# Stores and loads moved to another queue, one product and some sums moved in the order, and one tile given its own buffers, in a one-core encoder trunk

## The chip, the core and the metric

One core of one Trainium2 chip. The program runs alone on it. The metric is device time in microseconds (us) of one execution; below, "the runs" are repeated executions of the same program, and the trace is of one further execution, taken by the hardware profiler.

Names of engines: PE is the matrix engine (its clock is granted by a throttle, which the profile shows), DVE the vector engine, ACT the scalar engine, POOL GpSimd, SP the engine that only issues DMAs. POOL and ACT can issue DMAs too; a DMA stands in the instruction queue of the engine that issues it, in order with that engine's other work.

## The reference

Two groups of 512 tokens of width 1024 (`x_prompt`, `x_sample`) go through one encoder layer with shared weights. In short:

```python
h = rmsnorm(x, g_mix);  u = h @ w_in
qk, v, o, gates, c_q, c_kv, k_r, gm = split(u)          # gm: 2 x 1024 columns, the merge gates
y_m = (sigmoid(o) * rmsnorm(mlstm(qk, v, gates))) @ w_mo  # matrix memory, both directions
y_a = attention(rmsnorm(c_q) @ w_uq, rmsnorm(c_kv) @ w_ukv, k_r) @ w_ao   # 8 heads, rotary part
g_m, g_a = split(sigmoid(gm))
x = x + (g_m * y_m + g_a * y_a) @ w_out
h2 = rmsnorm(x, g_ffn)
x = x + (silu(h2 @ w_gate) * (h2 @ w_up)) @ w_down
x = x + sigmoid(x @ w_ple_gate) * (p @ w_ple)
y = rmsnorm(x, g_final)
```

All is float32.

## The kernel before

**Matmuls.** Data lie with the feature on the 128 partitions and the 512 tokens of a group along the free dimension. A float32 product is made of three matmuls: each operand is split into a high part (a cast, on ACT) and a low part (the rest, a subtraction, on DVE, line 168 in the helper `lo_of`), and high x high, high x low and low x high are summed in PSUM. So every operand costs one ACT instruction and one DVE instruction before PE can use it.

**Seven products for eight.** Where two column blocks of a weight meet the two groups, the kernel forms seven products of half the depth in place of eight (class `Seven`, lines 792 to 858). They are named P1, P2, P7, P6, P5, Q4, P3; each is 12 matmuls (lines 854 to 856). The weights of P7, P6 and P3 are sums of blocks, made by POOL in most places (lines 815 to 818 and 825). The products accumulate in banks b1 (P1, then P6, P5 and P3 on top), b0 (P2) and b2 (P7, then Q4). After P1, P6 and P5 ACT copies b1 (line 903); after P2, P5 and Q4 DVE combines the copy with b0 or b2 (line 908), and a finished result goes to `put`; P3's comes straight from b1.

**Order.** `chain` (lines 860 to 895) writes the order of the products of consecutive weight pairs; the dictionary `ends` holds it for the last pairs. A name with + belongs to the next pair. A hook runs right after a given product. In this part of the program a scheduler then sets each engine's order out of the program's.

**The stages.** (1) norm, input projections, mLSTM; (2) the merge gates, in pairs (`gate_pair`: column chunk c of the gates `gm` and `ga`); (3) latent attention in 16 half-heads (head, group), with one `hop` (operands of the mLSTM's output projection) prepared beside four half-heads; (4) the output projections and merging; (5) FFN; (6) per-layer embedding and the last norm. The order within the half-heads and within the last stage is written out by hand (`pinned[0] = True`); in the rest the scheduler decides.

**The end of stage 2.** Four gate pairs run in one `chain` with `two=True` and a hook (line 1258), pairs 0 to 3 there for chunks 4 to 7. Below, "pair 3" is the last and "pair 2" the one ahead of it. `gate_out` (line 1019) is their `put`: DVE multiplies by the norm's factor (line 1023), ACT takes the tanh (line 1024), and a DMA writes the tile `u` to `tmd` or `tad` in DRAM (line 1025). Three of a pair's four results stay in the tile that they were summed in; P3's is written to a fresh tile out of four rotating buffers (`ev4`), so its line 1023 waits until an earlier `u` in that buffer has been stored. The hook after pair 3's P6 is `first_unit` (line 1241): the projections for the first half-head, their rotary steps, and 16 small DMAs on SP that regroup them (`rot_put`, line 1111, tiles `qs`). After the chain come two loads of attention weights (`wa_load`, line 1070), the splits of the first of them, and the loads of the first hop's four tiles on POOL (line 718).

**A half-head.** `score(u, i)` forms one of four 128-query blocks (5 matmuls, bank `sc`), DVE takes the maximum (`mx`), ACT the exponential (`p`, line 1153 on), PE transposes it (`turn`, bank `pt`), ACT and DVE split the transposed block (`aph`, `apl`), and a half-head later PE multiplies it with the values (`weigh`, bank `av`). Between these stand work for the next half-head (projections `qn`, `kn`), the values' split (`vl`, on POOL), and slots filled from a dictionary `todo_` by the number of the half-head (lines 1305 to 1367): "mid" is ahead of the weighing, "e", "late" and "f" in its second half, "end" behind it. In the first half-head of each four, all three of P1's, P2's and P7's operands are prepared: `hop_hi` (ACT) and `hop_lo` (DVE), and for P7 a sum on DVE (`p7_sum`). The recorded instructions of this part all bear line 79.

**The end of the program.** The last stage's output of group 1's second half is in three parts of 4, 2 and 2 chunks of 256 tokens. `scaled` (line 1771) has ACT write x times the gain into a tile `xg`, ahead of time; `last_out` (line 1782) has DVE multiply it by the norm's factor and SP store it. All three `xg` are allocated from `WP`'s `wst`, which has two buffers.

Of the kernel before, what the change touches and what calls it, by code (L numbers as in the profile page):

```python
# [7 lines left out]
F32 = mybir.dt.float32  # L8
# [7 lines left out]
P = 128  # L16
# [4 lines left out]
KD = D // P  # L21
# [41 lines left out]
def encoder_kernel(ctx: ExitStack, tc: tile.TileContext, a):  # L63
    nc = tc.nc
# [233 lines left out]
    class Halves(Slots):  # L298
        n = 0
# [423 lines left out]
    late = {}  # L723
# [136 lines left out]
    def chain(quads, head=False, look=4, made=(), done=(), two=False, hook=None):  # L860

        order = [(0, n) for n in ("P1", "P2", "P7")]
        if head:
            order = [(0, "P1"), (0, "P2"), (1, "P1"), (1, "P2"), (0, "P7"), (0, "P6"), (0, "P5"), (0, "Q4"), (1, "P7"), (0, "P3")]
        full = ("P6", "+P1", "P5", "+P2", "Q4", "+P7", "P3")
        ends = {
            len(quads) - 3: ("P6", "+P1", "P5", "+P2", "Q4", "P3"),
            len(quads) - 2: ("P6", "P7", "P5", "+P1", "Q4", "P3"),
            len(quads) - 1: ("P6", "P7", "P5", "P2", "Q4", "P3"),
        }  # L870
        if two:
            order = [(0, "P1"), (0, "P2"), (1, "P1"), (1, "P2")]
            order += [(i, n) for n in ("P7", "P6", "P5") for i in (0, 1)]
            order += [(0, "Q4"), (0, "P3"), (2, "P1"), (1, "Q4"), (2, "P2"), (1, "P3")]
        for i in range(2 if two else 1 if head else 0, len(quads)):
            for n in ends.get(i, ("+P1", "+P2", "+P7", "P5", "Q4", "P3") if (i, "P6") in done else full):
                if n[0] != "+":
                    order.append((i, n))
                elif i + 1 < len(quads):
                    order.append((i + 1, n[1:]))  # L880
        made = dict(made)
        order = [o for o in order if o not in done]

        def make(i):
            if i not in made:
                made[i] = quads[i][1]()

        for at, (q, n) in enumerate(order):
            for i, m in order[at : at + look + 1]:
                quads[i][0].need(m)  # L890
            for i, _ in order[at : at + 2]:
                make(i)
            made[q].product(n)
            if hook and (q, n) in hook:
                hook[q, n]()
# [123 lines left out]
    def gate_out(c):  # L1019
        def put(at, t):  # L1020
            g = at[1]
            o = ev4("u") if at == (0, 1) else t
            V.tensor_tensor(out=o, in0=t, in1=rs1[0], op=ALU.mult)
            S.activation(out=o, in_=o, func=AF.Tanh, scale=0.5)
            nc.sync.dma_start((tmd, tad)[at[0]][g][c], o)

        return put

# [36 lines left out]
    NU = len(halves_)  # L1065
    was, wload, qn, kn, vn, vts, rots, rsteps, qst, att = ({} for _ in range(10))

    def wa_load(hd):
        wload[hd] = WP("wst", "wst", F32, (P, 1024))
        nc.sync.dma_start(wload[hd][:, 0:768], a["wa"][hd])  # L1070

    QK, RO = slice(256, 768), slice(0, 256)

# [187 lines left out]
    AX = Slots("AX", "right", rt=4, hs=4)  # L1261
    LOW.update(b1=("l0", None, None), b2=("l1", None, None))
    banks("P2", dict(sc=3, tp=2, av=1), sc="sc b0", tp="pt", av="av")
    wa_load(0)
    wa_split(0, QK)
    wa_load(1)
    hlo = {}

    def hop_load(k):
# [25 lines left out]
    for u in range(NU + 1):  # L1295
# [49 lines left out]
        if (more and r == 3) or (m == 3 and r == 1):  # L1345
# [11 lines left out]
            if more:  # L1357
# [2 lines left out]
                todo_["f"] = [(wa_lo, 2 * m + 3, QK)]  # L1360
                todo_["end"] = [(rot_put, m + 1, 1)]

        if u == 13:
            todo_["late"] = [(ahead_hi, "P1")]
            todo_["f"] = [(ahead_lo, "P1")]
# [402 lines left out]
                ob.rearrange("p (c t) -> p c t", c=per),  # L1768
            )

    def scaled(g, cs, b0, nb):

        n = nb * P
        xg = WP("wst", "xg", F32, (P, 1024))[:, 0 : len(cs) * n]
        for i, c in enumerate(cs):
            S.activation(
                out=xg[:, i * n : (i + 1) * n], in_=x2[g][c][:, b0 * P : b0 * P + n], func=AF.Copy,
# [51 lines left out]
    spread3(1, 0, H0)  # L1829
    first = rs2[1]  # L1830
    embed(KD - 1, 1, bk[3], toks[1], bps[1], True)
    gained = [(cs, scaled(1, cs, H0, H0)) for cs in (range(0, 4), range(4, 6), range(6, 8))]
    finish(1, [0, 1], 0, H0)
    sums(1, H0, H0)
    inv(1, H0)
# [116 lines left out]
```

## Time and profile before

| | us |
|---|---|
| median of 3 runs | 1861.39 |
| lowest and highest run | 1859.47, 1864.44 |
| the profiled execution, its own time | 1858.46 |
| its span in the trace | 1856.7 |
| mean granted PE clock | 0.994 |

How to read it: in the list of waits, "PE pt L79 <- ACT p L79: 4.1, 1, 4.1" says that PE's instruction with output pt stood idle for ACT's instruction with output p, 4.1 us in all, once, 4.1 us at the longest. A row of a timeline has start, duration, engine, line, operation, output<-input, shapes and count; the bracket at its end is the idle time of that engine just before, and what ended it. Durations of PE's matmuls overlap, so the distance of two starts tells their pace, not the duration. Rows that hold several like instructions (x4) give the duration of all of them. In the table of stretches each engine has its busy us and count of instructions, then the granted PE clock (1.00 is full), the DMA engines' busy share and GB/s.

PE is busy nearly all the time (98% of the span, 1815.0 us). Of the other 41.7 us, 14 lie in the last 17 us of the program and 4.9 between 600 and 645 us, where stage 2 passes into stage 3; the rest is in short pieces.

### The profile page before, as it was taken

To read this page: it belongs to the slowest core of one execution; us is meant where nothing else is said; L and a number is where in the kernel's file an instruction comes from. 1 tells how busy PE (TensorE), PEld (TensorE's weight loads), DVE (VectorE), ACT (ScalarE), POOL (GpSimd) and SP (SyncE) were. 2 spreads that over 40 slices of the span, in tenths; PEclk is the share of its full clock that TensorE was granted. 3 is DMA by queue.
4 is the path that set the end of the run, shared out by engine and by line. 5 is a ranking of instruction groups with operands and counts; after the bars stand their busy time and mean duration, and the time that the engine had idled before them with its cause. 6 is when DMAs were issued, how large, how long until landed. Compare 5 with 4: busy or idle time off the path is not lost.

```text
span 1856.7 us, 24624 instructions
## 1 busy us (share of the span) xinstructions
PE 1815.0 (98%) x8767; PEld 1514.7 (82%) x8767; DVE 1284.7 (69%) x2172; ACT 891.3 (48%) x1748; POOL 418.1 (23%) x340
## 2 busy tenths in 40 slices
PE   9999999999999899999999999999999999999996
PEld 7889898988877788877877888888888887888786
DVE  7757575767767777778897587444444469978656
ACT  6255555654454566664544355333333354534333
POOL 0100010110032122213130004665566523111000
PEclk9999999999999999999999999999999999999998
DMA  4211212123353443356565241322223246533232
GB/s 167 67 58 52 68 46 77 39 88 111 133 174 122 147 126 109 91 199 232 166 215 169 100 162 68 115 101 97 97 91 134 94 167 224 177 124 106 99 131 97
DMA packets 105243, 224.65 MB, mean 121 GB/s; under 512 B 12840, under 2 KB 23520, under 8 KB 105120
## 3 DMA queue, kind: packets, MB, share of 16 engines
q1 hardware_dynamic: 86864, 160.91, 25.9%
q10 hardware_dynamic: 13248, 47.19, 7.5%
q0 software_dynamic: 5008, 14.98, 2.5%
q8 instruction: 69, 1.13, 0.3%
q14 instruction: 54, 0.44, 0.1%
HBM read 164.57 MB, written 54.26 MB: 118 GB/s over the span
## 4 chain that ended last, share of the span: by engine, by line
PE 82%; DVE 10%; issue 3%; DMA 2%; ACT 2%; SPq 0%; POOL 0%; ACTq 0%; DVEq 0%; POOLq 0%
PE b L854 12%; PE b L856 12%; PE b L855 12%; PE mm L197 6%; PE mm L198 6%; PE mm L199 6%; PE sc L79 4%; PE mm L79 3%; PE nm L645 3%; PE l L79 3%; PE av L79 2%; DVE xl L168 2%; PE mm L565 2%; PE mm L564 2%; PE mm L563 2%
## 5 line engine op out<-in xcount | busy, mean ns | idle before, releaser
L854 PE MATMUL b<-xh,wp 128*128 128x512 f32 x1072 | 410.3, 391 | 9.3 <-ACT u L903 3.8
L855 PE MATMUL b<-xl,wp 128*128 128x512 f32 x1072 | 416.2, 389 | 0.8 <-DVE xl L168 0.8
L856 PE MATMUL b<-xh,wp 128*128 128x512 f32 x1072 | 413.1, 389 | 2.8 <-DVE wp L168 2.8
L788 ACT CAST wp<-wst 128x512 fp32r<-128x512 f32 (+1 forms) x289 | 175.9, 613 | 293.7 <-PE b L856 240.7
L168 DVE TENSOR_TENSOR wp<-wst,wp 128x512 fp32r<-128x512 f32 (+1 forms) x289 | 247.8, 860 | 71.5 <-ACT wp L788 71.3
L854 PEld LDWEIGHTS b<-xh,wp 128*128 128x128 f32 x1072 | 201.2, 188 | 56.9 <-ACT u L903 7.2
L856 PEld LDWEIGHTS b<-xh,wp 128*128 128x128 f32 x1072 | 201.2, 188 | 46.3 <-DVE wp L168 4.1
L855 PEld LDWEIGHTS b<-xl,wp 128*128 128x128 f32 x1072 | 201.2, 188 | 42.7 <-DVE xl L168 1.2
L197 PE MATMUL mm<-hh,whi 128*128 128x512 f32 x432 | 169.6, 393 | 0.0
L198 PE MATMUL mm<-hl,whi 128*128 128x512 f32 x432 | 169.2, 392 | 0.0
L199 PE MATMUL mm<-hh,wlo 128*128 128x512 f32 x432 | 168.9, 392 | 0.0
L908 DVE TENSOR_TENSOR u<-b,u 128x512 f32<-128x512 f32 x95 | 65.4, 690 | 136.9 <-PE b L856 83.4
L815 POOL TENSOR_TENSOR s<-wst,wst 128x512 f32<-128x512 f32 (+1 forms) x33 | 55.7, 1687 | 342.5 <-DMA wst<-w 117.9
L1640 POOL TENSOR_TENSOR sg<-sg,u 128x512 f32<-128x512 f32 x30 | 55.4, 1847 | 202.4 <-DVE u L908 202.4
L903 ACT COPY u<-b 128x512 f32<-128x512 f32 x93 | 52.6, 588 | 94.8 <-PE b L856 69.3
L199 PEld LDWEIGHTS mm<-hh,wlo 128*128 128x128 f32 x432 | 81.5, 189 | 17.1 <-DVE wlo L168 0.3
L182 ACT CAST whi<-wst 128x1024 fp32r<-128x1024 f32 x53 | 55.7, 1050 | 82.7 <-PE mm L198 40.7
L198 PEld LDWEIGHTS mm<-hl,whi 128*128 128x128 f32 x432 | 81.6, 189 | 16.5
L197 PEld LDWEIGHTS mm<-hh,whi 128*128 128x128 f32 x432 | 81.5, 189 | 16.5 <-DVE to L405 0.2
L168 DVE TENSOR_TENSOR xl<-ld,xh 128x512 fp32r<-128x512 f32 x105 | 80.4, 793 | 0.9 <-ACT xh L1671 0.8
L168 DVE TENSOR_TENSOR wlo<-wst,whi 128x1024 fp32r<-128x1024 f32 (+2 forms) x56 | 67.7, 1209 | 15.0 <-ACT whi L182 14.6
L611 POOL TENSOR_TENSOR b<-b,mask 128x512 f32<-128x512 f32 x16 | 25.5, 1595 | 222.5 <-DMA b<-nmd 179.3
(444 smaller groups left out, 3997.7 us busy)
## 6 DMA issues: line engine op xcount, KB each, us to landing
wst<-w ACTq DMA_DIRECT2D x68, 512.0 KB, 3.3
wst<-w SPq DMA_DIRECT2D x65, 512.0 KB, 3.3
ld<-actd SPq DMA_DIRECT2D x77, 256.0 KB, 3.0
actd<-t SPq DMA_DIRECT2D x40, 256.0 KB, 2.9
x<-x SPq DMA_DIRECT2D x32, 256.0 KB, 4.0
wst<-wd ACTq DMA_DIRECT2D x16, 512.0 KB, 3.2
actd<-sg SPq DMA_DIRECT2D x30, 256.0 KB, 2.1
ld<-hzd SPq DMA_DIRECT2D x28, 256.0 KB, 4.9
```

The costliest lines, as they stand in the source:

```text
L79: r = f(*args, **kw)
L168: e.tensor_tensor(out=out, in0=src, in1=hi.bitcast(F32), op=ALU.subtract)
L182: S.copy(hi[:, :n], st[:, :n])
L197: E.matmul(bk, whi[:, c], hi, start=k == 0, stop=False)
L198: E.matmul(bk, whi[:, c], lo, start=False, stop=False)
L199: last_mm[0] = E.matmul(bk, wlo[:, c], hi, start=False, stop=k == nk - 1)
L645: E.matmul(bk, l, r, start=n == 0, stop=n == len(terms) - 1)
L788: S.copy(hi, src)
L854: E.matmul(bk, whi[:, c], hi, start=bool(first) and k == 0, stop=False, **sk)
L855: E.matmul(bk, whi[:, c], lo, start=False, stop=False, **sk)
L856: E.matmul(bk, wlo[:, c], hi, start=False, stop=k == self.kh - 1, **sk)
L908: V.tensor_tensor(out=t, in0=b, in1=t, op=ALU.add if name == "P2" else ALU.subtract)
```

## The change

The work is the same; instructions are moved, none is added or taken away. Five edits:

1. The stores of the gates' last two chunks (c of 6 and 7, pairs 2 and 3: eight stores) are issued from POOL's queue, not from SP's.
2. The two loads of attention weights that stand behind the chain (`wa_load(0)` and `wa_load(1)`) are issued from POOL's queue too. That of `first_unit` stays on SP.
3. In `chain`, where there is a hook (this chain alone), pair 3's P6 stands ahead of pair 2's P3 rather than behind it, and with it its hook `first_unit`.
4. Of the first hop's operands, P1's are prepared in the second half of half-head 0, P2's in half-head 1 (with P7's sum), and P7's in half-head 2; the split of the weights for the rotary part (`wa_hi`, `wa_lo` with RO) moves from "mid" to "e" and "late" of half-head 0.
5. The second of the three last `xg` tiles comes from `WX`'s `wst`, so that the third finds a free buffer in `WP`.

```diff
@@ chain @@
+        if hook:
+            ends[len(quads) - 2] = ("P6", "P7", "P5", "+P1", "Q4", "+P6", "P3")
+            ends[len(quads) - 1] = ("P7", "P5", "P2", "Q4", "P3")
@@ gate_out @@
-            nc.sync.dma_start((tmd, tad)[at[0]][g][c], o)
+            (GP if c >= KD - 2 else nc.sync).dma_start((tmd, tad)[at[0]][g][c], o)
@@ wa_load @@
-    def wa_load(hd):
+    def wa_load(hd, q=nc.sync):
         wload[hd] = WP("wst", "wst", F32, (P, 1024))
-        nc.sync.dma_start(wload[hd][:, 0:768], a["wa"][hd])
+        q.dma_start(wload[hd][:, 0:768], a["wa"][hd])
@@ after the chain @@
-    wa_load(0)
+    wa_load(0, GP)
     wa_split(0, QK)
-    wa_load(1)
+    wa_load(1, GP)
@@ the half-heads @@
+        if u == 0:
+            todo_ = {
+                "e": [(wa_hi, 1, RO)],
+                "late": [(wa_lo, 1, RO), (hop_hi, "P1", hops.part("P1", 0)), (wa_hi, 1, QK)],
+                "f": [(hop_lo, "P1"), (wa_lo, 1, QK)],
+                "end": [(rot_proj, 1, 0)],
+            }
+        if u == 1:
+            todo_["mid"] = [(hop_hi, "P2", hops.part("P2", 0))]
+            todo_["e"] = [(hop_lo, "P2"), (p7_sum,)]
+        if u == 2:
+            todo_["mid"] = [(lambda: hop_hi("P7", p7[0]),)]
+            todo_["e"] = [(hop_lo, "P7")]
@@ scaled @@
-    def scaled(g, cs, b0, nb):
+    def scaled(g, cs, b0, nb, sl=WP):
 
         n = nb * P
-        xg = WP("wst", "xg", F32, (P, 1024))[:, 0 : len(cs) * n]
+        xg = sl("wst", "xg", F32, (P, 1024))[:, 0 : len(cs) * n]
@@ the end @@
-    gained = [(cs, scaled(1, cs, H0, H0)) for cs in (range(0, 4), range(4, 6), range(6, 8))]
+    gained = [
+        (cs, scaled(1, cs, H0, H0, sl)) for cs, sl in ((range(0, 4), WP), (range(4, 6), WX), (range(6, 8), WP))
+    ]
```

What becomes of POOL's queue, where edits 1 and 2 put their DMAs. The names: `wst` of line 825 holds the blocks of pair 3's weights (the sum is P3's), `ld<-hzd` are the first hop's loads, `vl` is the low part of the first half-head's values. Before, from pair 3's sums on:

```order
L818 TENSOR_TENSOR wst_6095<-wst_6095,wst_6097 128x512
L825 TENSOR_TENSOR wst_6095<-wst_6095 128x512
L718 DMA ld_6392<-hzd_0_780 128x512
L718 DMA ld_6394<-hzd_4_784 128x512
L718 DMA ld_6396<-hzd_0_788 128x512
L718 DMA ld_6398<-hzd_4_792 128x512
L79 TENSOR_TENSOR vl_6449<-avt_6400,vh_6448 128x512
```

and in the changed kernel, to the first of the hop's loads (three more of them, the store of `tmd_7_4767<-u_6372` and `vl` follow):

```order
L818 TENSOR_TENSOR wst_6095<-wst_6095,wst_6097 128x512
L1028 DMA tmd_6_4758<-u_5969 128x512
L1073 DMA wst_6384<-wa 128x768
L1028 DMA tad_6_4782<-u_6114 128x512
L1028 DMA tad_6_4774<-u_6080 128x512
L1073 DMA wst_6390<-wa 128x768
L1028 DMA tad_7_4783<-u_6311 128x512
L825 TENSOR_TENSOR wst_6095<-wst_6095 128x512
L1028 DMA tmd_6_4766<-u_6279 128x512
L1028 DMA tad_7_4775<-u_6179 128x512
L1028 DMA tmd_7_4759<-u_6136 128x512
L718 DMA ld_6392<-hzd_0_780 128x512
```

Six DMAs now stand between the sum for P6 and the sum for P3 of pair 3, and ten DMAs of the change in all stand ahead of `vl`.

DVE's queue where stage 3 begins. `u_6372` is the fresh tile for pair 3's P3; `mx` is the maximum over a block of scores, `u_6136` P2's result of pair 3, `wp` a weight's low part. Before:

```order
L908 TENSOR_TENSOR u_6311<-b_962_6283,u_6311 128x512
L1023 TENSOR_TENSOR u_6311<-u_6311,rs_64_348 128x512
L908 TENSOR_TENSOR u_6199<-b_962_6283,u_6199 128x512
L1023 TENSOR_TENSOR u_6199<-u_6199,rs_64_348 128x512
L1023 TENSOR_TENSOR u_6372<-b_934_6123,rs_64_348 128x512
L79 TENSOR_REDUCE mx_6402<-sc_6405 128x1
L79 TENSOR_TENSOR ld_6396<-ld_6396,ld_6398 128x512
L79 TENSOR_REDUCE mx_6402<-sc_6415 128x1
```

and in the changed kernel:

```order
L168 TENSOR_TENSOR wp_6357<-wst_6095,wp_6357 128x512
L1026 TENSOR_TENSOR u_6179<-u_6179,rs_64_348 128x512
L911 TENSOR_TENSOR u_6136<-b_966_6320,u_6136 128x512
L1026 TENSOR_TENSOR u_6136<-u_6136,rs_64_348 128x512
L1026 TENSOR_TENSOR u_6372<-b_934_6123,rs_64_348 128x512
L79 TENSOR_REDUCE mx_6402<-sc_6405 128x1
L79 TENSOR_REDUCE mx_6402<-sc_6414 128x1
L79 TENSOR_TENSOR ql_6434<-l_987_6425,qh_6432 128x512
```

The result of pair 3's P5 (`u_6311`) has left this stretch, and with it its products: on PE the order from pair 3's P1 on was P5 of pair 2, P7 of 3, P3 of 2, P6 of 3 and Q4 of 2 (interleaved), the rotary projection, P2, the first half-head's projections, P5, P3 and Q4 of pair 3, scores; it is now P7 of 3, P5 of 2, P6 of 3, Q4 of 2 within the rotary projection, P5 of 3, P3 of 2 around the first half-head's projections, then Q4, P2 and P3 of pair 3, scores. P7's sum (`ld_6396`) no longer stands between the two maxima.

## The prediction

> **What bounds the kernel now.** I read the page first, for the shares of the engines, then the list of what PE waited for.
>
> ```profile
> span 1856.7 us, 24624 instructions
> PE 1815.0 (98%) x8767; PEld 1514.7 (82%) x8767; DVE 1284.7 (69%) x2172; ACT 891.3 (48%) x1748; POOL 418.1 (23%) x340
> ```
> ```profile
> PE pt L79 <- ACT p L79: 4.1, 1, 4.1
> ```
>
> PE is the bound: 41.7 us of the span are all that it is not busy. A change that adds no work can gain only where PE stands, and the longest single stand is one of 4.1 us, at the first half-head's first transposition. PE's timeline around it, from the first product at which the new order differs:
>
> ```profile
> 594.88 0.39 PE L854 MATMUL b<-x,wp 128*128 128x512 f32 x1
> ...
> 619.13 0.39 PE L856 MATMUL b<-x,wp 128*128 128x512 f32 x1
> 620.30 0.50 PE L854 MATMUL b<-ph,wp 128*128 128x512 f32 x1 [0.78 <-ACT u L903]
> ...
> 629.27 0.39 PE L79 MATMUL l<-ckvh,wlo 128*128 128x512 f32 x1
> 633.77 1.11 PE L79 MATMUL pt<-ident,p 128*128 128x128 f32 x4 [4.12 <-ACT p L79]
> ...
> 639.63 0.39 PE L79 MATMUL sc<-qh,qh 128*128 128x512 f32 x1
> ...
> 642.59 0.39 PE L79 MATMUL sc<-qh,qh 128*128 128x512 f32 x1
> ```
>
> From 594.88 to 619.13 run nine blocks of 12 matmuls without a break: 107 steps in 24.25 us, 0.227 us a matmul. Against that pace the stretch to 642.59 loses three times: at 620.30, 1.17 - 0.23 = 0.94 us; at 633.77, 4.50 - 0.23 = 4.27; and behind that, since the pace itself falls. From 639.63 to 642.59 stand 11 matmuls and four transposes (2.96 us, so 0.46 for the four); from 633.77 to 639.63 stand 11 matmuls and twice four transposes, 3.42 us at that pace, and they took 5.86: 2.44 lost. The table of stretches shows the clock as the reason:
>
> ```profile
> 625.00:630.00 5.00, 4.66 (x21) 3.53 (x19) 1.38 (x2) 0.63 (x1) 0.00 (x0) 1.00 0.47 116
> 630.00:635.00 5.00, 1.23 (x5) 1.23 (x6) 2.49 (x4) 2.18 (x6) 0.00 (x0) 0.71 0.96 320
> 635.00:640.00 5.00, 5.00 (x17) 3.96 (x17) 3.85 (x7) 4.23 (x10) 1.27 (x1) 0.61 0.68 241
> ```
>
> In all 0.94 + 4.27 + 2.44 = 7.65 us are to be had here. Who made PE wait is read backwards, on ACT, DVE and SP in turn:
>
> ```profile
> 619.14 0.63 ACT L1024 ACTIVATE u<-u 128x512 f32<-128x512 f32 x1 [0.16 <-DVE u L1023]
> ...
> 632.39 0.63 ACT L1024 ACTIVATE u<-u 128x512 f32<-128x512 f32 x1 [4.24 <-DVE u L1023]
> 632.94 0.69 ACT L79 ACTIVATE p<-sc,mx 128x512 f32<-128x512 f32 x1
> ...
> 635.59 1.15 ACT L79 CAST xh<-ld 128x512 fp32r<-128x512 f32 x2
> ```
> ```profile
> 631.62 0.69 DVE L1023 TENSOR_TENSOR u<-b,rs 128x512 f32<-128x512 f32 x1 [4.13 <-DMA tmd<-u]
> 632.23 0.68 DVE L79 TENSOR_REDUCE mx<-sc 128x1 f32<-128x512 f32 x1
> ```
> ```profile
> 618.49 2.48 SPq L1111 DMA_DIRECT2D qs<-rs  x4
> ...
> 627.97 0.59 SPq L1111 DMA_DIRECT2D qs<-rp  x1
> ...
> 629.23 0.45 SPq L1025 DMA_DIRECT2D tmd<-u  x1
> ```
>
> The exponential waits for the maximum, the maximum stands on DVE behind line 1023 (pair 3's P3 into its fresh tile), that waits for the buffer's earlier store, and this store stands on SP behind the sixteen `qs` DMAs (618.49 to 628.56, about 0.6 us each). Its tanh was done at 619.8 (the first of the ACT rows), so over 9 us of its wait are queue.
>
> **The change part by part.** *Edits 1 to 3* meet this place together. I lay the new order on the old trace's pace. From 594.88 to the first scores PE has 132 matmuls (nine products, and 24 matmuls of first_unit), so without a break they end at 594.88 + 132 x 0.227 = 624.8, where the old kernel began its scores at 625.87. The question is whether anything holds PE, and for that I follow the last sum on POOL, with these rows:
>
> ```profile
> 610.23 1.29 POOL L825 TENSOR_TENSOR wst<-wst 128x512 f32<-128x512 f32 x1 [18.49 <-DVE wp L168]
> 611.45 0.55 POOL L718 DMA_DIRECT2D ld<-hzd  x1
> ...
> 637.34 1.27 POOL L79 TENSOR_TENSOR vl<-avt,vh 128x512 fp32r<-128x512 f32 x1 [20.44 <-ACT vh L79]
> ```
> ```profile
> L1002 POOL DMA_DIRECT2D b<-x x4: 536/546/693, 414.1 to 549.5; - x4
> ...
> DMA to landing us min/median/max: 2.9/3.4/5.5
> ```
>
> P3 of pair 3 comes last: PE wants its weights at 624.8 - 12 x 0.227 = 622.1. Its sum on POOL now stands behind six DMAs, the last of them the store of pair 3's P5. That product ends at 594.88 + 72 x 0.227 = 611.2; ACT's copy, DVE's two operations (0.69 each) and ACT's tanh (0.63) would need 3 us, but the rotary steps and the other weights' splits stand between them, and counting these off in their order (0.6 us a DVE operation, ACT with its casts for the projections that end at 615.3) I get the tanh at about 617.7. Then the DMA's issue (0.55) and the sum (1.29): 619.6. ACT, busy until 619.8 with the tanh for pair 2's P3, casts by 620.4; DVE has the low part by 621.6. So POOL is in time by 0.2 us and the weights by 0.5: close, and I charge nothing for it but keep it for the range. The store of pair 3's P5 waits for nothing else; a load of attention weights ahead of it waits for the split of Q4's weights, at about 614.3, also in time.
>
> Then the fresh tile. In the changed program it takes the buffer of pair 2's P3 (not of pair 3's P2 as before). That tile's store is issued at 619.8 to 620.4 and lands, at 2.9 to 5.5 us from issue on POOL, between 622.7 and 625.3. PE ends P3 at 624.8; line 1023 runs from 625.0 or 625.3, the first scores end at 625.9, the maximum is there at 626.8, the exponential (0.69) at 627.6. PE, with ten matmuls of scores and six of a projection behind 624.8, asks for it at 628.4. The stand of 4.12 us is gone with 0.8 us to spare, and with it the lower clock; on this path nothing else is late then. The stand of 0.78 us goes too: there P3 waited for ACT's copy of P5, which stood right ahead of it, and now 48 matmuls (11 us) lie between P5 and P3. SP, free of the stores, issues the `qs` DMAs from about 615 (rotary steps done), the first needed ones landed by 621 against scores at 624.8.
>
> One rule of the Trainium skill speaks against edits 1 and 2: "SBUF — State Buffer", section "SBUF: two separate sides", says that GpSimd's DMAs wait for their descriptors while DVE holds a port that both share, and gives (section "A bandwidth-pool intuition that's wrong") about 620 ns alone against about 3100 ns beside a DVE copy. By the rule the issue would be an estimated 3.1 us and the gain would go (as in the fourth case below, which is worked out from rows). No slowing shows in the trace: the issues on POOL took 536 to 693 ns, and the one of 0.55 us at 611.45 stood beside this on DVE, which has two operands in SBUF:
>
> ```profile
> 611.11 3.07 DVE L1042 TENSOR_TENSOR rs<-rp,sin 64x512 f32<-64x512 f32 x4 [1.03 <-ACT rp L1089]
> ```
>
> I go by those rows.
>
> *Edit 4.* In half-head 0 PE now runs at full pace, and ACT and DVE lose the time that the stand gave them. Following them from 626.8 with the durations above, PE finds the third block's exponential 0.25 us early and the rotary weights 0.1 us early; with P2's and P7's casts and low parts and P7's sum still there (two casts, 1.15 us, and three DVE operations at 0.6) it would find them late, so this edit is what lets the gain through. I charge 0.5 us for the thin margins, 0 to 2 as the bounds. What moves into half-heads 1 and 2 is 1.2 us on DVE and 0.6 on ACT in the one, 0.6 each in the other. It is hidden by DVE's idle time at that slot:
>
> ```profile
> 654.32 0.69 DVE L79 TENSOR_REDUCE mx<-sc 128x1 f32<-128x512 f32 x1 [1.22 <-PE sc L79]
> ```
>
> That is as long as the two operations; without the cover it would cost up to 1.2 us in half-head 1. The products that read these operands run 13 half-heads later; P6's sum, in half-head 3, still finds P7's tile. The moved loads on SP and POOL have a half-head of room.
>
> *Edit 5.* The end of the program, on ACT, DVE and SP, and the stretches:
>
> ```profile
> 1842.01 2.48 ACT L79 ACTIVATE xg<-x,cols 128x256 f32<-128x256 f32 x6
> 1851.57 0.91 ACT L79 ACTIVATE xg<-x,cols 128x256 f32<-128x256 f32 x2 [7.07 <-DMA out<-xg]
> ```
> ```profile
> 1847.23 1.81 DVE L79 TENSOR_TENSOR xg<-xg,rbc 128x1024 f32<-128x1024 f32 x2
> 1852.51 0.69 DVE L79 TENSOR_TENSOR xg<-xg,rbc 128x512 f32<-128x512 f32 x1 [3.46 <-ACT xg L79]
> ```
> ```profile
> L1787 SPq DMA_DIRECT2D out<-xg x3: 372/372/372, 1848.5 to 1853.2; - x3
> ```
> ```profile
> 1851.00:1852.00 1.00, 0.00 (x0) 0.00 (x0) 0.00 (x0) 0.43 (x2) 0.00 (x0) 0.50 0.71 239
> ...
> 1854.00:1855.00 1.00, 0.00 (x0) 0.00 (x0) 0.00 (x0) 0.00 (x0) 0.00 (x0) 0.50 0.78 262
> ```
>
> ACT's last two copies waited 7.07 us until the first part's store had let go of the buffer. With a free one they follow the six (1844.5 to 1845.4), DVE's last multiplication follows the two (1849.0 to 1849.7), and SP issues the last store at 1849.7 rather than 1853.2: 3.5 us. But the DMA engines are busy with the first two parts until about 1851.7, and the last part's bytes take 0.8 us: 1852.5 where it was about 1854.8. So the gain is 2.3 us by the bytes, 3.5 by the issue; I take 2.5, nearer to the bytes. `WX`'s buffer is free: its last weights were split before 1827.
>
> **Sum.** 7.65 - 0.5 + 2.5 = 9.65 us off the profiled execution: 1858.46 to 1848.8. That execution is 2.93 us below the median of the three runs (1861.39), which themselves spread over 5 us; the same sum off the median gives 1851.7, and that is what I predict. What a measurement of this kernel can tell from no change is about 0.3%, 5.6 us.
>
> **The rivals.** *As forecast* (0.70): gains of 7.65 - 2 + 2.3 = 8 to 7.65 + 3.5 = 11 us, so 1850.2 to 1853.4.
>
> *A smaller stand stays* (0.17): POOL's sum comes 1 to 2 us late, or the chain of splits on DVE, which I have without a pause from 609 to 621, slips by as much. For it speaks that margins are 0.2 to 0.8 us and that DVE and POOL can hold each other up:
>
> ```profile
> 588.81 1.78 DVE L1023 TENSOR_TENSOR u<-u,rs 128x512 f32<-128x512 f32 x1
> ```
> ```profile
> 588.41 1.62 POOL L816 TENSOR_TENSOR wst<-wst 128x512 f32<-128x512 f32 x1
> ```
>
> The DVE operation took 1.78 us for 0.69. Against it: in the new stretch POOL has one such operation, not three. One to two such delays cost PE 1.1 to 2.2 us twice over (at P3's weights and at the first exponential): 2 to 5 us with part of the clock's 2.44, so a gain of 5 to 7.5, 1854 to 1857.
>
> *The last part gains nothing* (0.06), as the DMA engines may drain three parts no faster than now: 7.15 us, 1854.2.
>
> *POOL's queue becomes the bound, slower* (0.04). Ten more DMAs stand on POOL ahead of `vl`, which the first weighing needs. PE came to it 4.33 us behind half-head 1's first scores (642.59):
>
> ```profile
> 646.92 0.39 PE L79 MATMUL av<-aph,vl 128*128 128x512 f32 x1
> ```
>
> Those I expect at 634.8 (38 matmuls and three blocks of transposes behind 624.8, 8.6 + 1.4 us), so PE wants `vl` at about 639.1. At 0.55 us each the DMAs are done by 627.7 and nothing waits. Were the issue X long, the last store before the sum, the sum, eight more DMAs and `vl` itself would end at 617.7 + 9X + 2.6: PE waits from X = 2.1 on, nine for one, and loses 2.4 to the clock. At X = 3.1 that is 9 + 2.4 = 11.4 us against 9.65 gained, 1863; at X = 3.5 it comes out slower by over 0.3%, and at X = 4 it is some 10 us slower, 1871. The figure of "SBUF — State Buffer" would put this case at 1863. The rows of 536 to 693 ns and of 0.55 us speak against it.
>
> *No effect at the boundary* (0.03): the old stand returns by another store; 2.5 us, 1858.9.
>
> **Range and chances.** The first case, with the runs' own spread of about 2.5 us to each side, is 1848 to 1856. Reaching into the second and the third gives 1848 to 1857.5; what is left out is the slow case, the one without effect and the tails, under 2 in 10. Faster by over 0.3% is below 1855.8: nearly all of the first and third case (0.73) and a third of the second (0.05): 0.78. Within 0.3%: 0.18. Slower: 0.04.
>
> **What would show it.** Right: PE's row "pt<-ident,p" at the first half-head without a bracket of several us, the clock 1.00 throughout 620 to 640, scores from about 624.8, half-head 1 from about 635; the last store issued near 1842 (1849.7 less 7.65), no ACT wait on "out<-xg". Wrong: a bracket on PE's P3 (b<-ph) naming ACT's cast of POOL's sum; POOL DMA issues well above 0.6 us; PE waits in half-heads 1 and 2 that name xh or xl; or the same rows as here with the time unchanged.

## The result, and the profile after

The changed kernel took 1850.75 us in the median of five runs (1848.86 to 1853.57), the kernel before, run beside it, 1861.39 (1859.47 to 1864.44): a ratio of 0.9941, 95% interval 0.9926 to 0.9955, so 10.6 us faster. The prediction was 1851.7 us, range 1848.0 to 1857.5. The profiled execution took 1851.81 us. Its page:

```profile
span 1850.0 us, 24624 instructions
PE 1815.0 (98%) x8767; PEld 1513.7 (82%) x8767; DVE 1287.1 (70%) x2172; ACT 890.3 (48%) x1748; POOL 425.3 (23%) x350
```

Over the whole span PE is busy as long as before to the tenth, and this pair of executions lies 6.7 us apart. By what is changed it is more: up to the first place where PE's orders differ the new execution runs 2.42 us behind the old one, with the same instructions in the same order on PE. PE's timeline before and after, from pair 3's P1:

```profile
592.15 0.39 PE L854 MATMUL b<-hh,wp 128*128 128x512 f32 x1
```
```profile
594.58 0.39 PE L854 MATMUL b<-hh,wp 128*128 128x512 f32 x1
...
597.30 0.39 PE L854 MATMUL b<-x,wp 128*128 128x512 f32 x1
...
624.50 0.39 PE L854 MATMUL b<-ph,wp 128*128 128x512 f32 x1
...
627.22 0.39 PE L79 MATMUL sc<-qh,qh 128*128 128x512 f32 x1
...
630.85 0.60 PE L79 MATMUL pt<-ident,p 128*128 128x128 f32 x4
...
637.25 0.39 PE L79 MATMUL sc<-qh,qh 128*128 128x512 f32 x1
```

From 597.30 to the first scores at 627.22 stand 132 matmuls in 29.92 us, 0.227 us each: no break. P3 at 624.50 and the first transposition at 630.85 carry no bracket. Half-head 1 begins at 637.25. I call the way from pair 3's P1 to there "the stretch"; it serves as the yardstick of all that follows. It took 642.59 - 592.15 = 50.44 us before and takes 637.25 - 594.58 = 42.67: 7.77 us gained. PE was busy for 45.54 of the 50.44 us and is for all of the 42.67, so 4.90 us of the gain are idle time and 2.87 a faster pace. The granted clock stays full:

```profile
630.00:635.00 5.00, 5.00 (x28) 4.14 (x27) 2.96 (x5) 3.88 (x10) 1.83 (x2) 1.00 0.95 298
635.00:640.00 5.00, 5.00 (x28) 4.17 (x27) 4.53 (x8) 3.54 (x9) 0.00 (x0) 1.00 0.67 240
```

(Before: 0.71 and 0.61.) The chain that had to be in time, on POOL, ACT and DVE:

```profile
620.23 0.55 POOL L1028 DMA_DIRECT2D tad<-u  x1 [1.81 <-ACT u L1027]
620.80 1.30 POOL L825 TENSOR_TENSOR wst<-wst 128x512 f32<-128x512 f32 x1
622.53 0.56 POOL L1028 DMA_DIRECT2D tmd<-u  x1 [0.43 <-ACT u L1027]
...
627.73 2.22 POOL L718 DMA_DIRECT2D ld<-hzd  x4
```
```profile
622.14 0.62 ACT L788 CAST wp<-wst 128x512 fp32r<-128x512 f32 x1
...
629.28 0.69 ACT L79 ACTIVATE p<-sc,mx 128x512 f32<-128x512 f32 x1 [0.45 <-DVE mx L79]
```
```profile
623.19 0.68 DVE L168 TENSOR_TENSOR wp<-wst,wp 128x512 fp32r<-128x512 f32 x1
...
627.42 0.69 DVE L1026 TENSOR_TENSOR u<-b,rs 128x512 f32<-128x512 f32 x1 [1.30 <-PE b L856]
628.55 0.69 DVE L79 TENSOR_REDUCE mx<-sc 128x1 f32<-128x512 f32 x1 [0.44 <-PE sc L79]
```

The sum for P3 follows the store without a gap, ACT's cast follows the sum, the low part is there at 623.87 and PE asks at 624.50. Line 1026 into the fresh tile now waits for PE and no longer for a store.

At the end of the program ACT writes all eight pieces of `xg` in one go and SP issues the three parts without a wait; the row of sums ahead of them, before and after, gives the length of the tail:

```profile
1838.17 3.28 ACT L79 ACTIVATE xg<-x,cols 128x256 f32<-128x256 f32 x8
```
```profile
1844.63 1.96 SPq L1803 DMA_DIRECT2D out<-xg  x3
```
```profile
1842.15 0.83 PE L79 MATMUL ssc<-onesr,sq 128*128 128x2 f32 x6 [0.80 <-ACT sq L79]
```
```profile
1838.31 0.83 PE L79 MATMUL ssc<-onesr,sq 128*128 128x2 f32 x6 [0.80 <-ACT sq L79]
```

To the end of the span it was 1856.7 - 1842.15 = 14.55 us and is 1850.0 - 1838.31 = 11.69: 2.86 us gained. The two together are 10.6 us, what the medians say. That they meet to the tenth is luck: the medians' interval runs from 8.4 to 13.8 us, and against another execution with the old stretch (49.66 us, experiment 8 below) the two together are 9.9.

Between half-head 1 and this row the two executions differ by 1.5 us (1199.56 before, 1201.06 after), the other way. That is scatter, as the 2.42 us are: over the twelve traces of this document pair 3's P1 starts between 590.06 and 594.89, and the kernel of experiment 8, whose instructions between these two places are those of the kernel before, took 1202.59 us from the one to the other.

### The profile page after: what moved, and what is told of

Read it like the earlier page. It is cut to its first block, busy times and chain, and to the rows that moved or that the text cites. A ratio compares the mean times of both kernels' runs of the same rounds, so it can differ in the third digit from the quotient of the medians.

```text
span 1850.0 us, 24624 instructions
## 1 busy us (share of the span) xinstructions
PE 1815.0 (98%) x8767; PEld 1513.7 (82%) x8767; DVE 1287.1 (70%) x2172; ACT 890.3 (48%) x1748; POOL 425.3 (23%) x350
## 4 chain that ended last, share of the span: by engine, by line
PE 87%; DVE 8%; DMA 2%; issue 1%; ACT 1%; POOL 0%; SPq 0%; DVEq 0%; ACTq 0%
PE b L854 12%; PE b L856 12%; PE b L855 12%; PE mm L197 7%; PE mm L199 7%; PE mm L198 7%; PE sc L79 4%; PE mm L79 3%; PE nm L645 3%; PE l L79 3%; PE av L79 2%; DVE xl L168 2%; PE mm L565 2%; PE mm L564 2%; PE mm L563 2%; PE pt L79 2%
```

## The experiments

My theory was that three things belong together: a store's place in SP's queue, the order that gives the store time, and the load on half-head 0. The main rival was that one of them, the queue, is all. I undid each edit by itself in the changed kernel and made three of them by themselves in the kernel before. All ratios are to the kernel before, run on the same chip; the stretch is from each profiled execution (the kernel before had 50.44 in its own trace, and 49.66 in the trace of experiment 8, where this part is unchanged). Experiments 9 and 10 ran on another chip than 1 to 8.

The stretch is read as above, from the first `b<-hh` of pair 3's P1 to the first scores of half-head 1.

| | what | ratio (95%) | stretch, us |
|---|---|---|---|
| 5 | the changed kernel again | 0.9942 (0.9930 to 0.9954) | 42.67 |
| 1 | stores on SP again | 0.9978 (0.9967 to 0.9989) | 47.20 |
| 2 | old order of products | 0.9965 (0.9953 to 0.9977) | 44.58 |
| 3 | edit 4 undone | 0.9999 (0.9990 to 1.0007) | 51.72 |
| 4 | four more issues on POOL | 0.9978 (0.9970 to 0.9987) | 45.91 |
| 6 | before + edits 1, 2 | 0.9984 (0.9975 to 0.9994) | 47.08 |
| 7 | before + edit 4 | 1.0002 (0.9993 to 1.0011) | 49.65 |
| 8 | before + edit 5 | 0.9982 (0.9971 to 0.9993) | 49.66 |
| 9 | changed, P7's sum back | 0.9992 (0.9983 to 1.0002) | 52.19 |
| 10 | edit 4 undone, P7's sum later | 0.9977 (0.9966 to 0.9989) | 48.25 |

**1. Edits 1 and 2 undone.**

```diff
-            (GP if c >= KD - 2 else nc.sync).dma_start((tmd, tad)[at[0]][g][c], o)
+            nc.sync.dma_start((tmd, tad)[at[0]][g][c], o)
-    wa_load(0, GP)
+    wa_load(0)
-    wa_load(1, GP)
+    wa_load(1)
```

> The changed kernel with edits 1 and 2 undone: the last gates' stores and the two loads of attention weights are on SP's queue again, while PE, ACT and DVE keep the new order. Theory (SP's queue of sixteen qs DMAs is one half of the cause, the order the other): on the clock of the changed kernel's trace the qs DMAs last until about 627.6, the store of pair 2's P3 stands right behind them and lands at about 630.2, so line 1023 into the fresh tile runs at 630.3, the maximum is there at 631, the exponential at 632.4, where PE asks at 630.85: a stand of 1.5 us at the first transposition, up to 4 with lateness behind it and the clock. So 1852.3 to 1855 us. Rival (the queue is everything): the whole 7.65 us come back, 1858.4. Second rival (the new order alone frees the tile): nothing comes back, 1850.8.

1855.86 us in the median of 11 runs; the stretch loses 4.53 us. On SP's queue, DVE, PE and in the table of stretches:

```profile
624.30 0.59 SPq L1114 DMA_DIRECT2D qs<-rp  x1
624.98 0.53 SPq L1028 DMA_DIRECT2D tmd<-u  x1
```
```profile
628.70 0.69 DVE L1026 TENSOR_TENSOR u<-b,rs 128x512 f32<-128x512 f32 x1 [5.48 <-DMA tmd<-u]
```
```profile
630.86 0.66 PE L79 MATMUL pt<-ident,p 128*128 128x128 f32 x4 [2.75 <-ACT p L79]
```
```profile
630.00:635.00 5.00, 4.14 (x16) 3.46 (x17) 2.75 (x5) 3.75 (x10) 1.27 (x1) 0.68 0.83 255
```

The chain is the one I named, store behind the last `qs`, fresh tile, maximum, exponential, PE; the store landed 3.7 us behind its issue where I had reckoned 2.6, so the stand is 2.75 us and not 1.5, and the clock costs 1.8 more. The new order alone does not free the tile; that rival is out. By the stretch the queue alone is not all either (4.5 of 7.8).

**2. Edit 3 undone.**

```diff
-        if hook:
-            ends[len(quads) - 2] = ("P6", "P7", "P5", "+P1", "Q4", "+P6", "P3")
-            ends[len(quads) - 1] = ("P7", "P5", "P2", "Q4", "P3")
```

> The changed kernel with edit 3 undone: the products of the last two pairs in the old order, the stores still on GpSimd's queue. Theory: the stand of 0.78 us at pair 3's P3 behind its P5 comes back (0.94 us against the pace), the one of 4.12 us does not, since the fresh tile's store no longer stands behind the qs DMAs: 1851.7 to 1853. Rival (the order is what frees the tile): the stand of 4.12 us and the lower clock come back as well, 7.65 us, 1858.4.

1853.4 us; the stretch loses 1.91 us. PE's stands, and how long the `qs` DMAs took to land (608 to 634):

```profile
620.82 0.50 PE L854 MATMUL b<-ph,wp 128*128 128x512 f32 x1 [0.79 <-ACT u L903]
...
627.55 0.50 PE L79 MATMUL sc<-kh,qs 128*128 128x512 f32 x1 [0.52 <-DMA qs<-rp]
```
```profile
DMA to landing us min/median/max: 5.3/5.3/5.3
```

The stand at P3 is back (0.79 us, before 0.78), the one of 4.12 is not, and the rival falls. A second stand, of 0.52 us, I had not seen: in the old order the `qs` DMAs begin 7.4 us ahead of the scores (619.00 and 626.41; before 618.49 and 625.87), which was enough when they landed in 1.9 to 2.0 us, as in the kernel before, and is not at 5.3 us, with the gates' stores out at the same time and the DMA engines full (1.02 of 1 in 625 to 630).

**3. Edit 4 undone.** The block `if u == 0: ... if u == 2: ...` of the diff is left out.

> The changed kernel with edit 4 undone: casts, low parts and the sum for P2 and P7 are in half-head 0 again; PE's and POOL's orders stay. Theory (this edit lets the gain through): P7's sum stands on DVE between the first two maxima, and its inputs are loaded on POOL behind the stores, landing at 631 to 633 on the changed kernel's clock, so that the second maximum and its exponential are 2 to 3 us late and ACT and DVE have no pause in which to make it up: 3 to 5 us lost, 1854 to 1856. Rival (edit 4 is covered, the margins are wider than I had them): no change, 1850.8.

1859.66 us: the whole gain of the boundary is gone and more, the stretch of 51.72 us is longer than before any edit. I had 3 to 5 us. The place is the one named, the size is not:

```profile
633.71 0.69 DVE L79 TENSOR_TENSOR ld<-ld,ld 128x512 f32<-128x512 f32 x1 [8.05 <-DMA ld<-hzd]
```
```profile
635.87 1.11 PE L79 MATMUL pt<-ident,p 128*128 128x128 f32 x4 [6.84 <-ACT p L79]
```

DVE stands 8.05 us in P7's sum for its loads, with the second block's maximum behind it. That made two explanations of edit 4 compete: too much work in half-head 0 (the prediction's), or one operation that waits for late loads. Experiments 9 and 10 part them.

**9. One instruction put back.** P7's sum alone stands between the two maxima again; on PE, ACT and POOL the order is that of the changed kernel.

```diff
         if u == 0:
             todo_ = {
+                "a": [(p7_sum,)],
                 "e": [(wa_hi, 1, RO)],
...
-            todo_["e"] = [(hop_lo, "P2"), (p7_sum,)]
+            todo_["e"] = [(hop_lo, "P2")]
```

> The changed kernel with one instruction put back: P7's sum (one DVE operation of 0.69 us) stands between the first two maxima of half-head 0 again, as in the kernel before; its cast and low part, and all of P2, stay in half-heads 1 and 2. PE's, ACT's and POOL's orders are those of the changed kernel. Theory (what the third experiment lost was this sum's wait for its loads, which land only when the DMA engines have drained, some 9 us behind their issue): the stand at the second transposition is 5 to 7 us again, the clock falls behind it, the boundary stretch is 7 to 9 us longer, and the time 7 to 10 us above the changed kernel's: ratio to before 0.998 to 1.000. Rival (half-head 0 has too much work for ACT and DVE, which was the prediction's reason for this edit): 0 to 0.7 us lost, ratio 0.9942 to 0.9946.

1860.45 us, 9.3 us above experiment 5 by the ratios; the stretch loses 9.52. One operation of 0.69 us costs that. PE, DVE, POOL, then all that reads or writes `ld` from 615 to 645:

```profile
634.83 1.11 PE L79 MATMUL pt<-ident,p 128*128 128x128 f32 x4 [6.74 <-ACT p L79]
```
```profile
632.67 0.69 DVE L79 TENSOR_TENSOR ld<-ld,ld 128x512 f32<-128x512 f32 x1 [7.94 <-DMA ld<-hzd]
```
```profile
623.22 2.22 POOL L718 DMA_DIRECT2D ld<-hzd  x4
```
```profile
DMA to landing us min/median/max: 6.0/7.0/7.7
```

The same line for the kernel before, from 605 to 655, and the table of stretches of experiment 9 (the last two columns are the DMA engines' share and GB/s):

```profile
DMA to landing us min/median/max: 2.9/3.0/3.5
```
```profile
628.00:630.00 2.00, 0.09 (x1) 0.00 (x0) 0.00 (x0) 0.00 (x0) 0.00 (x0) 1.00 0.97 335
630.00:632.00 2.00, 0.00 (x0) 0.00 (x0) 0.00 (x0) 0.00 (x0) 0.00 (x0) 0.54 1.02 402
632.00:633.00 1.00, 0.00 (x0) 0.00 (x0) 0.33 (x1) 0.00 (x0) 0.00 (x0) 0.50 0.58 225
```

So the wait has two parts. The loads are issued at 623.2 to 624.9, behind the stores on POOL, when DVE comes to the sum at 624.7; in the kernel before they were issued at 611.5 to 616.4, more than 16 us ahead of the sum. With 3.0 us to land DVE would have waited some 3 us. The other 5 are the DMA engines: stores, `qs` pieces and loads now fall together, the engines are full, and the loads land when they run empty, at 632.7.

**10. The work back, the sum later.** As experiment 3, but P7's sum stands behind P2's low part.

```diff
                 "f": [(hop_lo, "P7")],
             }
+            if m == 0:
+                todo_["e"].append(todo_.pop("a")[0])
             if more:
```

> As the third experiment (edit 4 undone, P2's and P7's work in half-head 0), but with P7's sum behind the low part of P2 and no longer between the first two maxima: the work in half-head 0 is all there, only the place of one DVE operation is another. Theory (loads that land late, not the amount of work): no stand at the second transposition; the casts of P1 and P2 on ACT stand ahead of the third block's exponential and need loads as well, so that 1 to 4 us of the stand come back there: 2 to 5 us lost at the boundary, ratio to before 0.995 to 0.998. Rival (amount of work): the loss of the third experiment's kind less the wait, spread over several small stands of up to 1 us, 1 to 3 us in all and none that names a load.

1856.49 us; the stretch loses 5.58 us, a little more than I expected. ACT and PE:

```profile
630.62 0.62 ACT L79 CAST xh<-ld 128x512 fp32r<-128x512 f32 x1 [1.81 <-DMA ld<-hzd]
...
632.62 0.62 ACT L79 CAST xh<-ld 128x512 fp32r<-128x512 f32 x1 [1.39 <-DMA ld<-hzd]
```
```profile
636.43 1.12 PE L79 MATMUL pt<-ident,p 128*128 128x128 f32 x4 [4.02 <-ACT p L79]
```

The wait moves to the next readers of the loads, P1's and P2's casts ahead of an exponential on ACT: 3.2 us in two pieces that name the loads, and a stand of 4.02 us on PE. So it is mostly the loads. The other 0.8 us fits the amount of work: ahead of the third block's exponential ACT has three casts here that the changed kernel has elsewhere (a `whi` and two `xh`), some 1.5 us, and in the changed kernel that exponential was done only 0.7 us before PE came to it (634.72 and 635.42).

**4. POOL's queue made longer.** Four further copies of one store, to tiles that nobody reads, ahead of the sum for P3.

```diff
+            if at == (1, 1) and c == KD - 1:
+                for d in scr:          # four DRAM tiles
+                    GP.dma_start(d, o)
```

> The changed kernel with four further copies of the store of pair 3's P5, to places that nobody reads, issued on GpSimd's queue right behind it and so ahead of the last sum of weights. ACT's cast and DVE's low part of these weights come one and three places later in their orders. Theory (issues take 0.55 us each, the sum had 0 to 0.6 us to spare): the sum ends 2.2 us later, at 624.3 on the changed kernel's clock, the cast at 624.9, the low part at 625.6 to 626.3, PE asks at 624.5: a stand of 0.5 to 1.5 us at pair 3's P3, no drop of the clock, and everything behind it later by as much: 1851.3 to 1852.5. Rival (an issue on this queue takes about 3.1 us beside DVE's work): 12.4 us later, a stand of about 11 us and the clock behind it, 1862 to 1865. Second rival (POOL has more than 2 us to spare): no change, 1850.8, and no bracket at P3.

1855.51 us; the stretch loses 3.24 us. POOL, DVE, ACT and PE (line numbers are one to four higher here):

```profile
620.54 0.55 POOL L1029 DMA_DIRECT2D tad<-u  x1 [1.80 <-ACT u L1028]
621.08 2.14 POOL L1032 DMA_DIRECT2D scr<-u  x4
623.24 1.30 POOL L826 TENSOR_TENSOR wst<-wst 128x512 f32<-128x512 f32 x1
```
```profile
623.55 1.54 DVE L1027 TENSOR_TENSOR u<-u,rs 128x512 f32<-128x512 f32 x1
```
```profile
626.99 0.60 ACT L789 CAST wp<-wst 128x512 fp32r<-128x512 f32 x1
```
```profile
627.65 0.50 PE L855 MATMUL b<-ph,wp 128*128 128x512 f32 x1 [2.68 <-ACT wp L789]
```

Four issues took 2.14 us, 0.53 each, in the midst of DVE's densest work. The rival with 3.1 us an issue is out. The one with 2 us to spare had no bracket at P3, where the stand is 2.68 us. It is larger than my 0.5 to 1.5 because the scheduler put the cast two places later on ACT, where I had one: it stands behind two tanhs, both of which were late, and starts at 626.99, 2.45 us after the sum was done. DVE's operation ahead of the first tanh took 1.54 us for 0.69, beside POOL's sum. So the edit changed two things, and what the four issues alone would cost is not shown. Of the 6.7 us that the ratios show, the stretch of this one execution accounts for half; a further stand of 0.90 us, at 668.09, behind the stretch, names DVE's `ql` and is not in the changed kernel's trace.

**5. The changed kernel again.**

> The changed kernel itself once more, beside a run of the kernel before on the same chip, as the base for the other runs. Expected: the ratio of the first time, 0.994, within 0.0015; by the traces of the first four experiments (4.5, 1.9, 9.1 and 3.2 us lost at the boundary against medians that say some 2.3 to 3.5 us more), rather the upper end, 0.995. Rival (the medians are right and the edits undone cost something outside the boundary): 0.993 to 0.994.

1849.73 us beside 1861.07: 0.9942. The ratio is the first one again, close to the rival's range and not the 0.995 that I had leaned to, though the interval holds both. The medians of experiments 1 to 4 lie 6.7, 4.3, 10.6 and 6.7 us above it where their stretches account for 4.5, 1.9, 9.1 and 3.2. The first three differences are within their interval of about 3 us, the fourth (3.5) is not; that all four have one sign is not explained, apart from the clock (below). Experiments 9 and 10 lie 9.3 and 6.5 us above it, for 9.5 and 5.6 by their stretches.

**6. Edits 1 and 2 alone.**

```diff
-            nc.sync.dma_start((tmd, tad)[at[0]][g][c], o)
+            (GP if c >= KD - 2 else nc.sync).dma_start((tmd, tad)[at[0]][g][c], o)
-    wa_load(0)
+    wa_load(0, GP)
-    wa_load(1)
+    wa_load(1, GP)
```

> Edits 1 and 2 alone on the kernel before: the last gates' stores and two loads of attention weights on GpSimd's queue, all else as before. Theory (a store's queue and the first half-heads' load belong together): the stand of 4.12 us at the first transposition goes, but the loads for P7's sum now stand behind the stores and land only when the DMA engines have drained, so that a stand of about 6 us comes at the second transposition instead, with the clock behind it: 0 to 2 us slower than before. Rival (the queue alone is the cause): 4.27 + 2.44 us faster, the 0.94 us at P3 stays: 6.7 us faster.

1858.0 us, 3.0 faster; the stretch gains 3.4. Neither expectation holds. PE's stands and DVE's wait in the sum:

```profile
618.58 0.50 PE L854 MATMUL b<-ph,wp 128*128 128x512 f32 x1 [0.79 <-ACT u L903]
625.37 0.50 PE L79 MATMUL sc<-kh,qs 128*128 128x512 f32 x1 [0.58 <-DMA qs<-rp]
630.67 0.66 PE L79 MATMUL pt<-ident,p 128*128 128x128 f32 x4 [0.21 <-ACT p L79]
635.64 0.66 PE L79 MATMUL pt<-ident,p 128*128 128x128 f32 x4 [1.80 <-ACT p L79]
```
```profile
628.51 0.69 DVE L79 TENSOR_TENSOR ld<-ld,ld 128x512 f32<-128x512 f32 x1 [1.45 <-DMA ld<-hzd]
```

The stand of 4.12 us is gone, but four smaller ones stay. In the old order POOL reaches the loads at 619.6, 29.2 us behind pair 3's P1 at 590.43 (in experiment 9 it was 33.1, 623.2 against 590.06), and DVE comes to the sum some 2 us later (36.6 us behind that P1, 34.7 in experiment 9), so the sum waits 1.45 us and not 8. I had carried the wait of experiment 3 over to an order in which the loads come 4 us sooner and their reader 2 us later.

**7. Edit 4 alone.** The block of the diff, in the kernel before.

> Edit 4 alone on the kernel before: the casts, low parts and sum for P2 and P7 move out of half-head 0. Theory (it only keeps a gain that the stores make): the stand of 4.12 us stays, since the fresh tile's store still stands behind the qs DMAs, and what is taken off ACT and DVE was hidden by it or comes back in the products behind it: 0 to 1 us faster. Rival (this edit carries the gain by itself, as undoing it cost 9 us at the boundary): 5 to 9 us faster.

1861.74 us, no change. PE:

```profile
634.28 0.66 PE L79 MATMUL pt<-ident,p 128*128 128x128 f32 x4 [4.12 <-ACT p L79]
```

The same stand to the hundredth. Edit 4 gives nothing that can be told by itself; it keeps what edits 1 to 3 give.

**8. Edit 5 alone.** The line with `WX`, in the kernel before.

> Edit 5 alone on the kernel before: the last output part has a tile of its own from the other pool. Theory (independent of the boundary; the bytes and not the issue set the end): the tail from the last row of sums to the end goes from 14.5 to 11.7 us as in the changed kernel, 2.8 us faster, 0.9985, and no ACT wait on the store. Rival (the DMA engines drain three parts no faster): 0 us, the tail 14.5 us.

1857.66 us, 3.4 faster by the ratio (1.3 to 5.4). In the trace (span 1858.2, the row of sums at 1845.82) the tail takes 12.38 us, 2.2 less than before, and ACT writes `xg` without a wait. Over all traces the tail takes 14.19 to 14.55 us without edit 5 (three) and 11.69 to 12.38 with it (nine, seven of them at most 11.75). The term is 2.2 to 2.9 us, mostly near 2.8, and independent of the boundary.

## Why the prediction was right, and where it was not

**The old loss and its cause.** 7.65 us to be had at the boundary, in three pieces. The stretch gave 7.77. The cause, a store behind sixteen `qs` DMAs, is shown from both sides: put back on SP, it stands behind the last of them and the fresh tile waits for it (experiment 1), and taken off SP in the old order, the stand of 4.12 us goes (experiment 6). The third piece, 2.44 us for the clock, is what one execution lost: with the same stand of 4.12 us experiment 7 took 5.06 us from that transposition to the last block of scores where the kernel before took 5.86, so 1.64 lost, and the stretches of experiments 7 and 8 are 0.8 shorter. That the size fits as closely as it does is in part luck.

**The new chain.** Less the 2.42 us by which this execution runs behind, the rows of the changed kernel are, in the order of the prediction: tanh and issue 617.8 (predicted 617.7), sum done 619.7 (619.6), low part 621.5 (621.6), P3 wanted 622.1 (622.1), fresh tile 625.0 (625.0 or 625.3), maximum done 626.8 (626.8), exponential done 627.6 (627.6), PE asks 628.4 (628.4), half-head 1 at 634.8 (634.8). Counting instructions at the pace of rows from the old trace placed every one within 0.2 us.

**The charge of 0.5 us for thin margins in half-head 0** was not due: from the first scores to half-head 1 it took 10.03 us against 10.0. What moved into half-heads 1 and 2 cost nothing, as forecast: half-head 1 took 13.35 us before (642.59 to 655.94) and after (637.25 to 650.60), and PE has no stand in either half-head.

**POOL's margin.** The prediction gave the sum 0.2 us and kept a smaller stand as a rival with 0.17. The margin was there: the sum was done 2.4 us and the low part 0.6 us before PE asked. It was thin: in experiment 4 the sum was done 0.4 us before PE asked and PE stood for 2.68, though there with the cast later in ACT's order as well. That rival did not come about, but it was a near one.

**The slower rival** needed issues of 2.1 us and more. The changed kernel's eight stores took 0.54 to 0.56 us each on POOL, and experiment 4's copies 0.53. The Trainium skill's "SBUF — State Buffer" ("SBUF: two separate sides") ties the wait for descriptors to DVE's two-port modes, its example a float32 copy, and gives about 3.1 us beside such a copy ("A bandwidth-pool intuition that's wrong"); no run here shows it. In the traces of the boundary DVE has operations on two tensors and maxima, no copy, so the rival had carried the figure for a copy over to other operations, and the case that the page describes is not tested.

**Edit 4: right in effect, its reason only a small part.** The step reads that with P2's and P7's casts, low parts and the sum in half-head 0 PE "would find them late". I had summed the durations of the work, and that accounts for about 0.8 us (an estimate from experiment 10). What counts more is that this work reads loads which edits 1 to 3 push 16 us back in relation to their reader, into a time in which the DMA engines are full; the loads took 6.0 to 7.7 us to land (experiment 9; 6.2 to 8.9 in the changed kernel) where they had taken 2.9 to 3.5. Without the edit the boundary was slower than before (51.72 us, experiment 3), and the wait of a single instruction is enough for that (52.19, experiment 9). The prediction priced the moved loads as having "a half-head of room", which is so only because edit 4 moves their readers too.

**The last part.** 2.5 us predicted, 2.86 and 2.2 measured. Counted from the row of sums, the last store is issued 7.5 us behind it where it was 11.1 (1845.8 and 1853.2), 3.6 us earlier, and the end comes only 2.86 earlier; from that issue the DMA engines are full (1.03 and 1.04 of 1 from 1846 to 1848) until about 1848.6. So the bytes set it, as taken, and not the issue.

**The sum.** 7.77 + 2.86 = 10.6 us against 9.65, and 10.6 by the medians: 0.5 us of the difference is the charge that was not due, the rest the two other terms (0.12 and 0.36).

## What to carry to other kernels

When a store or a load is moved to another queue, follow the loads that now stand behind it to their first reader, and price them by the DMA engines' load at the new time, not by how long they took at the old: an in-order engine that reaches one such reader too soon stops for all of it. Edits that are worth little or nothing alone can carry one another (edits 1 and 2 alone 3.0 us, edit 4 none, edit 5 some 3, all five 10.6; edit 3 alone was not tried), so undoing one in the finished kernel and making one in the old are different questions. A chain counted in instructions at the trace's own pace is good to a few tenths of a microsecond; waits on a loaded resource are not.

## What the runs showed of the hardware

**The clock falls for pieces of 3.4 us.** Where the clock is down throughout a stretch, the tables show 0.50 (as in 632 to 633 of experiment 9). Time at half clock worked out from them: experiment 1 had 0.68 in 630 to 635 and 0.98 in 635 to 640, so (0.32 + 0.02) x 5 / 0.5 = 3.4 us; the kernel before had 0.71 and 0.61, so 6.8; experiment 3 had 0.82 and 0.50, 6.8; experiment 9 0.52, 0.50 and, in 640 to 645, 0.96, 10.2; experiment 7, with the same stand of 4.12 us as the kernel before, only 3.4:

```profile
630.00:635.00 5.00, 0.88 (x6) 0.72 (x6) 1.89 (x3) 2.10 (x6) 0.00 (x0) 0.98 0.96 295
635.00:640.00 5.00, 5.00 (x18) 4.04 (x18) 3.19 (x5) 3.40 (x8) 1.28 (x1) 0.68 0.83 285
```

One stand can thus cost one piece or more, the same stand one or two, and the prediction's 2.44 us was one draw. A stand of 2.75 us brought the clock down (experiment 1), one of 2.68 us did not (experiment 4, 1.00 throughout). The Trainium skill's "TensorE: Matmul & The Clock Gate", section "Part 1: The HAM clock gate", says that the clock is set by windows of 3.4 us that run on freely; the pieces agree. It also gives one idle window as the condition; here less than a window's idleness was enough.

**The spread of this kernel's runs goes with the clock.** Of the 29 runs of the kernel before beside experiments 1 to 4, the two with a mean granted clock of 0.991 took 1865.0 us in the mean, the eight with 0.993 1860.3, the three with 0.995 1858.3. An estimate from these figures: 0.004 x 1857 / 0.5 = 14.9 us more at half clock, at most 7.4 us lost, and 6.7 were measured. What brought the clock down in one run and not in another is not shown. The changed kernel's five runs of experiment 5 had 0.995 and 0.996. A stand that is long enough to bring the clock down in some executions and not in others, such as experiment 4's, would cost more in the median than one trace shows; that would fit its missing 3.5 us, but is only argued.

**Loads stretch under the DMA engines' load.** The four 256-KB loads on POOL landed 2.9 to 3.5 us behind their issue in the kernel before, and 6.0 to 7.7 us in experiment 9, where stores, `qs` pieces and other loads fell together and the engines were full (0.97 and 1.02 of 1 in its table). The 64-KB `qs` pieces went from 1.9 to 5.3 us in the same way (experiment 2), and to 3.1 in the changed kernel.
